# Gate and up products of two FFNs as seven block products each, with their result kept in DRAM until the down product

## The chip, the cores and the metric
One core of a Trainium2 chip runs the whole program in one launch. The metric is device time in microseconds. The kernel before took 2929.18 us (median of three runs, 2927.11 to 2929.26).

## The reference
Two transformer blocks on 1024 tokens of width 1024, all in float32. Each has a mixer (block 1: sliding-window attention and an mLSTM; block 2: retention and an indexed sparse attention), an output projection with norm and residual, and an FFN with a hidden width of 2816. Only the FFNs, and the projections that lead into them, are touched:

```python
# block 1
mix = merged @ w_out;  x = x + gate_m * rms_norm(mix, g_post_mix)
h2 = modulate(rms_norm(x, g_pre_ffn), shift_f, scale_f)
ff = (silu(h2 @ w_ffn_gate) * (h2 @ w_ffn_up)) @ w_ffn_down
x = x + gate_f * rms_norm(ff, g_post_ffn)
# block 2
h = h + rms_norm(mixed, g_post)
up = causal_dwconv(rms_norm(h, ffn_norm_pre) @ w_up, conv_w, conv_b)   # three taps along the tokens
g, u = split(up);  ffn = (silu(g) * u) @ w_down
h = h + rms_norm(ffn, ffn_norm_post)
```

## The kernel before
A dense product splits each float32 operand into two float32r parts (hi + lo) and adds hi*hi, hi*lo and lo*hi in one PSUM bank: three matmuls for each block of 128 contracted features (mm3, L129 to L133). Weights come from DRAM as units of 1 MB into one raw buffer; ScalarE copies the high part (L643) and GpSimd subtracts it to make the low part (L645), in pieces of 512 columns, some steps ahead of their use. There is one raw buffer, so the load of a unit (L631) waits for the last split of the unit before.

TensorE, VectorE, ScalarE and GpSimd each run their instructions in the order in which the program writes them ("steps": a slot emits its matmuls, and work put off from earlier slots is emitted between slots). DMAs are issued by SyncE, also in order. PSUM has four banks for products (pd), three (pa) for transposes and other results, and one more.

`dense` (L164) serves both blocks. The output projection goes slot by slot, 24 matmuls of 256 columns each: a slot is a unit of columns and a token block of 128. Once a token block has its four units, `residual` (L203) adds it to x (L209), squares it on ScalarE, takes a power on GpSimd (L148), and scales it (L217); in block 1 GpSimd then adds a shift row (L219). `turn` (L225) transposes the eight 128x128 blocks of a token block on TensorE (L157); ScalarE and VectorE split the result (L160, L161).

The FFN has 22 gate/up units of 128 gate and 128 up features. `gate_up` makes for each unit, for two halves of 512 tokens, the gate and the up product: 8 blocks x 3 matmuls of 512 columns each. In block 1 ScalarE takes the Silu (L304) and VectorE multiplies (L305); in block 2 `convolve` comes first, half by half, with two taps on VectorE (L295, L296). The hidden result is split (L306, L307) and stays in SBUF. After every two units follows `down`: 8 token blocks x 2 column halves x 6 matmuls, added to an accumulator in SBUF by VectorE (L338). So gate/up and down alternate. The ends of the phases (the last down groups, the norms, the projection of the next phase) are written out by hand.

Of the kernel before, what the change touches and what calls it, by code (L numbers as in the profile page):

```python
# [35 lines left out]
# Rows of the table of row vectors.  # L36
# [3 lines left out]
# Columns of the table of per-feature columns.  # L40
# [15 lines left out]
# 2 * pi in pieces: products of the first four with integers below 2 ** 16 are exact.  # L56
# [8 lines left out]
def pipeline(n, stages):  # L65
    """Emit stage k of item i together with stage 0 of item i + k, older items first (None: a step of delay)."""
# [6 lines left out]
class Steps:  # L73
    """Work put off to later steps of an emission loop."""
# [12 lines left out]
class Builder:  # L87
# [54 lines left out]
    def rstd(self, pool, ssum, n, width, eps=EPS):  # L142
        """(ssum / n + eps) ** -0.5 for a [P, width] tile."""
# [7 lines left out]
    def transpose_split(self, x, tbl, big, kt0, nkt):  # L151
        """nkt [P, P] blocks of x transposed into kt0.. of big [P, 2, KT, HALF] at token block tbl."""
# [11 lines left out]
    def dense(self, pool, bigs, held, w0, names, x_src, x_mid, x_dst, rows, rows2, conv, ahead=None):  # L164
        """x_mid = x_src + norm(X @ W) * row; x_dst = x_mid + norm(down(act(gate, up))) * row, a step at a time.

        held: results of the output projection's first unit that are in PSUM already.  ahead: (unit of weights,
        function) of the next phase's first projection, which covers the end of this phase; the unit after it.
        Returns the next norm's transposed parts and the weights of that unit."""
        nc = self.nc  # L170
        steps = Steps()
        W = {("o", i): w for i, w in enumerate(w0)}
# [1755 lines left out]
```

## Time and profile before

| | us |
|---|---|
| median of three runs | 2929.18 |
| the profiled execution: span from the first to the last instruction | 2928.6 |
| TensorE busy in it | 2816.4 |
| VectorE, ScalarE, GpSimd busy in it | 1347.1, 1084.4, 1183.2 |

Of the profiled execution the profile gives the span; the runs are timed apart, and their median is 0.6 us above it. The output projection of block 1 runs from about 730 to 809 us of the span and its FFN to about 1537; those of block 2 from about 2123 to 2195 and to the end. In the profile PE is TensorE's matmuls, PEld its weight loads, DVE VectorE, ACT ScalarE, POOL GpSimd and SP SyncE. A busy PE means that matmuls are in flight, not that each is at its peak rate. A line L645 is line 645 of the kernel; helpers such as mm3 have the lines of many callers.

### The profile page before, as it was taken

Reading aid. Unit: us, or ns where it says so; the run is one execution under the profiler, and the core shown is the slowest. Engines: PE = TensorE matmul, PEld = TensorE weight load, DVE = VectorE, ACT = ScalarE, POOL = GpSimd, SP = SyncE. Lnnn points to the kernel's source line nnn. Section 1 sums busy time; section 2 is a strip of 40 time slices with the busy share of each in tenths; the row PEclk is TensorE's granted clock in tenths of the full one; section 3 lists DMA queues with packets and bytes.
Section 4 is the critical chain, followed back from the end, with each engine's and each line's share of the span. In section 5 each row is a group of like instructions: output and inputs, shape, how many; then the busy total and the mean of one; then the engine's idle time right before and its main releaser. Section 6 shows DMA issues by size and latency. Waiting matters only on the chain. (4 is left out here: it accounts for less than half of the span.)

```text
span 2928.6 us, 41049 instructions
## 1 busy us (share of the span) xinstructions
PE 2816.4 (96%) x16152; PEld 2441.9 (83%) x16152; DVE 1347.1 (46%) x2618; ACT 1084.4 (37%) x2294; POOL 1183.2 (40%) x1217
## 2 busy tenths in 40 slices
PE   5899999999999999999998999989999999999999
PEld 4898888888978888888878999978897888888887
DVE  8645434532522222111135787786444444444446
ACT  5653213232331111111123767747534322333333
POOL 5652222244443322232346444568433433333345
PEclk7999999999999999999999999999999999999999
DMA  6112343253321111111123111111131111111113
GB/s 206 39 36 103 105 165 105 96 192 130 116 94 58 57 44 44 43 46 56 44 79 108 44 43 41 49 58 45 52 124 58 51 58 44 44 43 58 44 44 144
DMA packets 67815, 220.15 MB, mean 75 GB/s; under 512 B 7159, under 2 KB 26615, under 8 KB 53542
## 3 DMA queue, kind: packets, MB, share of 16 engines
q1 hardware_dynamic: 67622, 217.53, 21.1%
q8 instruction: 127, 2.08, 0.3%
q14 instruction: 66, 0.54, 0.1%
HBM read 183.93 MB, written 33.57 MB: 74 GB/s over the span
## 5 line engine op out<-in xcount | busy, mean ns | idle before, releaser
L645 POOL TENSOR_TENSOR wlo<-raw,whi 128x512 fp32r<-128x512 f32 (+1 forms) x426 | 570.1, 1358 | 375.9 <-ACT whi L643 375.1
L131 PE MATMUL pd<-big,whi 128*128 128x512 f32 x1792 | 703.5, 393 | 0.0
L133 PE MATMUL pd<-big,wlo 128*128 128x512 f32 x1792 | 698.0, 390 | 1.7 <-POOL wlo L645 1.7
L132 PE MATMUL pd<-big,whi 128*128 128x512 f32 x1792 | 697.5, 389 | 0.0
L131 PE MATMUL pd<-whi,big 128*128 128x256 f32 (+1 forms) x1728 | 504.1, 292 | 8.0 <-ACT whi L643 3.6
L132 PE MATMUL pd<-wlo,big 128*128 128x256 f32 (+1 forms) x1728 | 494.2, 286 | 8.2 <-POOL wlo L645 8.2
L133 PE MATMUL pd<-whi,big 128*128 128x256 f32 (+1 forms) x1728 | 493.1, 285 | 0.9 <-POOL big L582 0.6
L133 PEld LDWEIGHTS pd<-big,wlo 128*128 128x128 f32 x1792 | 336.4, 188 | 73.2 <-POOL wlo L645 2.6
L131 PEld LDWEIGHTS pd<-big,whi 128*128 128x128 f32 x1792 | 336.6, 188 | 70.0 <-issue 1.2
L132 PEld LDWEIGHTS pd<-big,whi 128*128 128x128 f32 x1792 | 336.6, 188 | 70.0 <-issue 1.4
L307 POOL TENSOR_TENSOR hid<-sg,hid 128x512 fp32r<-128x512 f32 x88 | 113.9, 1295 | 619.1 <-ACT hid L306 619.1
L132 PEld LDWEIGHTS pd<-wlo,big 128*128 128x128 f32 x1728 | 335.8, 194 | 10.9 <-POOL wlo L645 9.9
L131 PEld LDWEIGHTS pd<-whi,big 128*128 128x128 f32 x1728 | 335.3, 194 | 11.4 <-ACT whi L643 4.5
L133 PEld LDWEIGHTS pd<-whi,big 128*128 128x128 f32 x1728 | 335.2, 194 | 1.4 <-POOL big L582 0.9
L338 DVE TENSOR_TENSOR big<-big,pd 128x512 f32<-128x512 f32 x304 | 206.3, 686 | 176.2 <-PE pd L133 176.1
L132 PE MATMUL pd<-wlo,hid 128*128 128x512 f32 x704 | 277.6, 394 | 0.0
L131 PE MATMUL pd<-whi,hid 128*128 128x512 f32 x704 | 276.8, 393 | 0.0
L133 PE MATMUL pd<-whi,hid 128*128 128x512 f32 x704 | 273.5, 388 | 0.0
L643 ACT ACTIVATE whi<-raw 128x512 fp32r<-128x512 f32 (+1 forms) x428 | 246.0, 621 | 15.9 <-DMA raw<-in_wu 15.9
L305 DVE TENSOR_TENSOR sg<-sg,pd 128x512 f32<-128x512 f32 x44 | 30.2, 687 | 432.9 <-PE pd L133 432.9
L295 DVE SCALAR_TENSOR_TENSOR cv<-craw,cols,cv 128x512 f32<-128x512 f32 x88 | 87.3, 992 | 290.4 <-ACT cv L294 187.1
L289 ACT ACTIVATE craw<-pd 128x512 f32<-128x512 f32 x88 | 52.7, 599 | 351.1 <-PE pd L133 349.4
(375 smaller groups left out, 3986.7 us busy)
## 6 DMA issues: line engine op xcount, KB each, us to landing
raw<-in_wu SPq DMA_DIRECT2D x109, 1024.0 KB, 4.9
row<-in_w_ada SPq DMA_DIRECT2D x32, 512.0 KB, 3.8
x_d<-xin SPq DMA_DIRECT2D x24, 512.0 KB, 2.6
ada<-in_w_ada SPq DMA_DIRECT2D x16, 512.0 KB, 8.0
xin<-x_d SPq DMA_DIRECT2D x16, 512.0 KB, 3.3
big<-in_x SPq DMA_DIRECT2D x8, 512.0 KB, 4.8
tga_d<-tg SPq DMA_DIRECT2D x16, 256.0 KB, 2.2
tgm_d<-tg SPq DMA_DIRECT2D x16, 256.0 KB, 2.0
```

What stands on the lines that cost most here:

```text
L131: mm(ps, lh, rh, start=start, stop=False)
L132: mm(ps, lh, rl, start=False, stop=False)
L133: mm(ps, ll, rh, start=False, stop=stop)
L289: nc.scalar.activation(raw[:, 2:], ps, AF.Copy)
L295: nc.vector.scalar_tensor_tensor(cv, raw[:, 1 : 1 + HALF], wc[1], cv, op0=ALU.mult, op1=ALU.add)
L305: nc.vector.tensor_mul(sg, sg, u)
L307: nc.gpsimd.tensor_tensor(out=lo, in0=sg, in1=hi.bitcast(F32), op=ALU.subtract)
L338: nc.vector.tensor_add(a, a, ps)
L643: nc.scalar.activation(w[0][:, c], raw[:, c], AF.Copy)
L645: eng.tensor_tensor(out=w[1][:, c], in0=raw[:, c], in1=w[0][:, c].bitcast(F32), op=ALU.subtract)
```

## The change
The tokens are taken as even and odd token blocks, the 1024 contracted features as two halves, the outputs as gate and up. That makes 2 x 2 blocks, whose product Winograd's form of Strassen's method needs in seven block products in place of eight. Weights keep their unit of 1 MB, but laid out as four quarters.

* `combine` makes in place, for a pair of token blocks, the four combinations of the tokens' side; `turn_block` transposes and splits one block of one of the seven left operands (a pair has seven such blocks of four transposes each). They are emitted in the last slots of the output projection and the first of the FFN. Combinations of the first three pairs are GpSimd's, of the last VectorE's. Some go through DRAM (`t_d`).
* `prep` makes one of the seven weight operands of a unit: sums on VectorE, the high part on ScalarE, the low part on GpSimd or (three of seven in block 2) VectorE. Operands are made up to six slots ahead.
* `multiply` makes one product, 4 x 3 matmuls of 512 columns. Products 1 and 2 share a PSUM bank (A), as do 6, 7 and 4 (B), and 5 and 3 (Z): later ones are added to the earlier. `after_product` (emitted at the start of the next slot) takes what the bank holds then.
* The first unit makes products 1, 3 and 2 in two halves of 256 columns, and uses one more bank.
* In block 2 the convolution runs over all 1024 tokens of the unit before.
* The hidden result goes to DRAM (`h_d`). All down groups follow after the last unit; each loads its two hidden blocks and splits them.

```diff
+        def combine(p, eng):
+            e, o = yrow[2 * p], yrow[2 * p + 1]
+            e1, e2, o1, o2 = e[:, :HALF], e[:, HALF:], o[:, :HALF], o[:, HALF:]
+            for out, a, b in ((e1, o1, e1), (o1, o2, o1), (o2, o2, e1), (e2, e2, o2)):
+                eng.tensor_tensor(out=out, in0=a, in1=b, op=ALU.subtract)
...
+        def prep(f, m, eng):
...
+            def total(a, b, op):
+                t = px.tile([P, HALF], F32, tag="ws", bufs=3, name="ws")
+                nc.vector.tensor_tensor(out=t, in0=a, in1=b, op=op)
+                return t
+            if m in (6, 5, 3) and (f, 5) not in sums:
+                sums[f, 5] = sub(a21, a22, ALU.add)
+                sums[f, 6] = sub(sums[f, 5], a11)
+            if m == 3:
+                sums[f, 3] = sub(a12, sums[f, 6])
+            if m == 7:
+                sums[f, 7] = sub(a11, a21)
...
+            nc.scalar.activation(w[:, 0], s, AF.Copy)
+            eng.tensor_tensor(out=w[:, 1], in0=s, in1=w[:, 0].bitcast(F32), op=ALU.subtract)
...
+        def multiply(f, m, c, special):
+            b = {1: "A", 2: "A", 6: "B", 7: "B", 4: "B", 5: "Z", 3: "Y" if special else "Z"}[m]
...
+        def after_product(f, m, special, c):
...
+            if m == 1:
...
+                nc.scalar.activation(t["t1"][:, c], A[:, c], AF.Copy)
+            elif m == 6:
+                t["u2"] = temp()
+                plus(t["u2"], t["t1"], B)
...
+            elif m == 7:
+                t["w"] = temp()
+                plus(t["w"], t["t1"], B)
+                if conv:
+                    plus(odd(raws[1][:, 2:]), four(t["w"]), four(Z))
+                else:
+                    plus(t["w"], t["w"], Z)
...
+            elif m == 2:
+                if conv:
+                    nc.scalar.activation(even(raws[0][:, 2:]), four(A), AF.Copy)
+                else:
+                    t["sg"] = temp()
+                    nc.scalar.activation(t["sg"], A, AF.Silu)
+            elif m == 3 and not special:
+                c12(f)            # u2 + Z: to raws[0], or (block 1) in place and Silu
+                if not conv:
+                    product(f, 1)     # on GpSimd, and to DRAM
+            elif m == 4:
+                if conv:
+                    plus(even(raws[1][:, 2:]), four(t["t1"]), four(B))
+                else:
+                    plus(t["t1"], t["t1"], B)
+                    product(f, 0)     # on VectorE, and to DRAM
...
+        def conv_taps(f, j):
...
+            for i in (1, 0):
+                nc.vector.scalar_tensor_tensor(cv, raws[j][:, i : i + S], wc, cv, op0=ALU.mult, op1=ALU.add)
+            if j == 0:
+                nc.scalar.activation(cv, cv, AF.Silu)
...
+        order = (1, 6, 5, 7, 2, 3, 4)
...
+        for f in range(1, NF):
+            pre = [[] for _ in range(7)]
+            if conv:
+                g = f - 1
+                pre[0] += [lambda g=g: conv_start(g, 0)]
+                pre[1] += [lambda g=g: conv_taps(g, 0), lambda g=g: conv_start(g, 1)]
+                pre[2] += [lambda g=g: conv_taps(g, 1)]
+                pre[3] += [lambda g=g: conv_end(g)]
...
+                pre[0] += [q(f, 3, v if conv else nc.gpsimd), q(f, 4)]
+            if f + 1 < NF:
+                pre[1] += [lambda f=f: raw_load(f + 1)]
+                for i in range(5):
+                    pre[2 + i] += [q(f + 1, order[i], v if conv and i in (2, 4) else nc.gpsimd)]
...
+            run([slot(f, m, pre[i]) for i, m in enumerate(order)])
```

In a slot of this loop, first what follows on the product before is emitted, then the entries of `pre`, then the slot's matmuls. `q` is `prep`, with GpSimd for the low part unless another engine is given.

## Rows read from the trace of the kernel before

**Rows 1.** The page: busy time of TensorE, its busy tenths, and its granted clock.
```profile
PE 2816.4 (96%) x16152; PEld 2441.9 (83%) x16152; DVE 1347.1 (46%) x2618; ACT 1084.4 (37%) x2294; POOL 1183.2 (40%) x1217
...
PE   5899999999999999999998999989999999999999
...
PEclk7999999999999999999999999999999999999999
```
**Rows 2.** Busy time by stretches: bounds, length, each engine's busy us, clock, DMA.
```profile
773.00:809.00 36.00, 28.65 (x239) 27.70 (x237) 27.97 (x37) 14.13 (x36) 18.93 (x16) 1.00 0.39 147
809.00:835.00 26.00, 22.06 (x108) 17.73 (x107) 16.57 (x21) 12.33 (x24) 16.06 (x11) 1.00 0.46 162
1098.00:1171.00 73.00, 73.00 (x323) 60.26 (x322) 15.63 (x23) 11.29 (x20) 20.19 (x16) 1.00 0.13 44
2195.00:2222.00 27.00, 24.15 (x118) 19.76 (x117) 16.93 (x25) 15.24 (x29) 9.47 (x15) 1.00 0.28 98
2342.00:2416.00 74.00, 74.00 (x327) 61.06 (x326) 33.58 (x43) 21.11 (x36) 24.39 (x30) 1.00 0.16 57
```
**Rows 3.** Instructions in order of time, VectorE, first FFN: start, length, what.
```profile
1002.29 0.69 DVE L305 TENSOR_TENSOR sg<-sg,pd 128x512 f32<-128x512 f32 x1 [10.19 <-PE pd L133]
1013.17 0.69 DVE L305 TENSOR_TENSOR sg<-sg,pd 128x512 f32<-128x512 f32 x1 [10.19 <-PE pd L133]
```
**Rows 4.** In order of time, TensorE, end of the second output projection.
```profile
2187.16 1.04 PE L157 MATMUL pa<-ident,big 128*128 128x128 f32 x8
2187.95 0.36 PE L131 MATMUL pd<-whi,big 128*128 128x256 f32 x1
...
2193.78 1.04 PE L157 MATMUL pa<-ident,big 128*128 128x128 f32 x8
```
**Rows 5.** In order of time, GpSimd, second FFN.
```profile
2263.81 2.99 POOL L645 TENSOR_TENSOR wlo<-raw,whi 128x512 fp32r<-128x512 f32 x2
...
2272.38 5.06 POOL L645 TENSOR_TENSOR wlo<-raw,whi 128x512 fp32r<-128x512 f32 x4 [0.21 <-ACT whi L643]
...
2403.28 5.08 POOL L645 TENSOR_TENSOR wlo<-raw,whi 128x512 fp32r<-128x512 f32 x4
...
2435.89 2.54 POOL L645 TENSOR_TENSOR wlo<-raw,whi 128x512 fp32r<-128x512 f32 x2
...
2438.51 2.99 POOL L645 TENSOR_TENSOR wlo<-raw,whi 128x512 fp32r<-128x512 f32 x2
```
**Rows 6.** In order of time, GpSimd, first turn into the FFN.
```profile
802.01 2.43 POOL L219 TENSOR_TENSOR big<-big,row 128x1024 f32<-128x1024 f32 x1 [1.50 <-DVE big L217]
```
**Rows 7.** Groups by line and shape, whole span: count, busy us, mean ns, idle before.
```profile
L643 ACT ACTIVATE whi<-raw 128x512 fp32r<-128x512 f32 x424 | 243.8, 621 | 15.9 <-DMA raw<-in_wu 15.9
L294 ACT ACTIVATE cv<-pd,cols 128x512 f32<-128x512 f32 x88 | 68.2, 775 | 0.0
L148 POOL TENSOR_TENSOR rs_r<-rs_v,mhalf 128x1 f32<-128x1 f32 x56 | 35.5, 641 | 77.1 <-DVE rs_v L146 77.1
L304 ACT ACTIVATE sg<-cv 128x512 f32<-128x512 f32 x44 | 27.8, 632 | 0.0
L198 ACT ACTIVATE junk<-xin 128x1024 bf16<-128x1024 f32 x24 | 25.4, 1057 | 39.8 <-DVE xin L209 35.3 <-DVE rs_v L146 4.3
```
**Rows 8.** In order of time, VectorE, end of the kernel.
```profile
2892.01 0.69 DVE L395 TENSOR_TENSOR yout<-big,row 128x512 f32<-128x512 f32 x1
...
2894.10 2.41 DVE L384 SCALAR_TENSOR_TENSOR big<-yout,rs_r,big 128x1024 f32<-128x1024 f32 x1
...
2898.96 1.29 DVE L384 SCALAR_TENSOR_TENSOR big<-yout,rs_r,big 128x1024 f32<-128x1024 f32 x1
```
**Rows 9.** In order of time, VectorE, second FFN.
```profile
2401.03 2.50 DVE L338 TENSOR_TENSOR big<-big,pd 128x512 f32<-128x512 f32 x4
2404.21 0.69 DVE L338 TENSOR_TENSOR big<-big,pd 128x512 f32<-128x512 f32 x1 [0.69 <-PE pd L133]
...
2438.60 1.76 DVE L295 SCALAR_TENSOR_TENSOR cv<-craw,cols,cv 128x512 f32<-128x512 f32 x1 [4.70 <-POOL craw L288]
2440.39 1.66 DVE L296 SCALAR_TENSOR_TENSOR cv<-craw,cols,cv 128x512 f32<-128x512 f32 x1
2442.51 0.75 DVE L295 SCALAR_TENSOR_TENSOR cv<-craw,cols,cv 128x512 f32<-128x512 f32 x1 [0.45 <-ACT cv L294]
```
**Rows 10.** In order of time, GpSimd, end of the kernel.
```profile
2894.12 1.31 POOL L395 TENSOR_TENSOR yout<-big,row 128x512 f32<-128x512 f32 x1
...
2899.04 2.38 POOL L395 TENSOR_TENSOR yout<-big,row 128x512 f32<-128x512 f32 x1
```
**Rows 11.** In order of time, SyncE's queue, second FFN.
```profile
2266.83 10.96 SPq L631 DMA_DIRECT2D raw<-in_wu  x2
```
**Rows 12.** In order of time, ScalarE, second FFN.
```profile
2271.67 2.20 ACT L643 ACTIVATE whi<-raw 128x512 fp32r<-128x512 f32 x4 [0.88 <-DMA raw<-in_wu]
```

More of the change, by code (lines that the diff above doesn't have):

```diff
@@ new lines, in dense @@
+        banks, tt = {}, {}
+        even = lambda x: x.rearrange("p (b e t) -> p b e t", e=2, t=P)[:, :, 0]
+        odd = lambda x: x.rearrange("p (b e t) -> p b e t", e=2, t=P)[:, :, 1]
+        four = lambda x: x.rearrange("p (b t) -> p b t", t=P)
+        def multiply(f, m, c, special):
+            b = {1: "A", 2: "A", 6: "B", 7: "B", 4: "B", 5: "Z", 3: "Y" if special else "Z"}[m]
+            first = (f, b) not in banks or special and m in (1, 3)
+            if (f, b) not in banks:
+                banks[f, b] = self.ps() if b == "B" else self.pd()
+            ps, w, x = banks[f, b], wq[f, m], X[m]
+            for k in range(4):
+                lh, ll = w[:, 0, k * P : (k + 1) * P], w[:, 1, k * P : (k + 1) * P]
+                for i, (l, r) in enumerate(((lh, x[:, 0, k, c]), (lh, x[:, 1, k, c]), (ll, x[:, 0, k, c]))):
+                    nc.tensor.matmul(ps[:, c], l, r, start=first and k == 0 and i == 0, stop=k == 3 and i == 2, skip_group_check=True)
@@ new lines, in c12, with product @@
+        def c12(f):
+            t, Z = tt[f], banks[f, "Z"]
+            if conv:
+                plus(odd(raws[0][:, 2:]), four(t["u2"]), four(Z))
+            else:
+                plus(t["u2"], t["u2"], Z)
+                nc.scalar.activation(t["u2"], t["u2"], AF.Silu)
+        def product(f, o):
+            t = tt[f]
+            h, u = (t["u2"], t["w"]) if o else (t["sg"], t["t1"])
+            (nc.gpsimd if o else nc.vector).tensor_tensor(out=h, in0=h, in1=u, op=ALU.mult)
+            nc.sync.dma_start(h_d[f, :, o * HALF : (o + 1) * HALF], h)
@@ L260, in dense, with conv_end @@
+        def conv_end(f):
+            g, u = tt[f]["cv", 0], tt[f]["cv", 1]
+            nc.vector.tensor_tensor(out=g, in0=g, in1=u, op=ALU.mult)
+            nc.sync.dma_start(h_d[f], g)
         for tb, ps in held.items():
@@ new lines, in dense, with slot, body @@
+        calls[3, 6] = [lambda: combine(1, nc.gpsimd), q(0, 3)]
+        calls[3, 7] = [d(3, 2), d(1, 2)]
+        run([(lambda s=s: ([fn() for fn in calls.get(s, ())], proj(*s)())) for s in slots])
+        lo, hi = slice(0, 256), slice(256, HALF)
+        post = []
+        def slot(f, m, pre=(), c=slice(0, HALF), special=False):
+            def body():
+                for fn in post:
+                    fn()
+                post.clear()
+                for fn in pre:
+                    fn()
+                multiply(f, m, c, special)
+                post.append(lambda: after_product(f, m, special, c))
+            return body
@@ new lines, in dense, with hid_piece, first_hidden @@
+        eso.close()
+        if conv:
+            pools["v"] = self.pool(eso, name + "v")
+        order = (1, 6, 5, 7, 2, 3, 4)
+        groups, hidden = {}, {}
+        def hid_piece(f, c, hraw, eng):
+            hi, lo = (hidden[f][:, i, c * HALF : (c + 1) * HALF] for i in range(2))
+            s = hraw[:, c * HALF : (c + 1) * HALF]
+            nc.scalar.activation(hi, s, AF.Copy)
+            eng.tensor_tensor(out=lo, in0=s, in1=hi.bitcast(F32), op=ALU.subtract)
+        def first_hidden():
+            t = self.bigtile([P, 4, 2, S], F32R)
+            for i in range(4):
+                hidden[i] = t[:, i]
@@ L405, in dense @@
             fetch("dn", g[1], (2, 2, 3, 3))
-            run([lambda tb=tb: both(g[:1], tb) for tb in range(4)] + [lambda tb=tb, c=c: slot(tb, c) for tb in range(NT) for c in range(2)])
+            run([lambda tb=tb: both(g[:1], tb) for tb in range(4)] + [lambda tb=tb, c=c: last(tb, c) for tb in range(NT) for c in range(2)])
+            eso.close()
             return None, None
@@ L441, in dense @@
         assert not steps.due
+        eso.close()
         return nxt, W[then]
```

300 lines of the change are left out of this document (200 added, 100 removed).

## The prediction
> **What bounds the kernel now.** I read the page first. TensorE is busy for 96% of the span, and its row of forty slices shows 9s nearly throughout [rows 1]. Then the busy time by stretches: in the middle of either FFN, TensorE is busy for the whole stretch, while VectorE has 15.6 of 73 us in the first FFN and 33.6 of 74 in the second, ScalarE 11 to 21 and GpSimd 20 to 24 [rows 2]. So an FFN lasts as long as its matmuls are many, and the other engines seem to have room. Where an output projection turns into an FFN there is idle time on TensorE: 7.4 and 3.9 us in the two stretches around the first turn, 2.9 us at the second [rows 2]. The granted clock is 1.00 (of 2.4 GHz) in all five stretches, so I leave it out of the sum. The question is whether the change keeps the other engines off TensorE's path.
>
> **Matmuls removed.** A gate/up unit has 2 x 2 x 8 x 3 = 96 matmuls of 512 columns now. Two halves of a unit start 10.88 us apart [rows 3], so 48 matmuls take 10.88 us, 0.2267 each. After the change a unit has 7 x 4 x 3 = 84, that is 19.04 us for 21.76: 2.72 us less. For 44 units: **-119.7 us**. The down product's matmuls stay as many.
>
> **Matmuls added.** The transposes grow from 64 to 7 x 4 x 4 = 112 for each FFN. Eight take 0.79 us [rows 4], so 96 more cost **+9.5**. The first unit does three products in two halves of 256 columns; such a matmul takes 0.12 us (48 and a start-up in 5.83 us [rows 4]): 72 x 0.12 - 36 x 0.2267 = 0.5 for each FFN, **+1**.
>
> **The turns into the FFNs.** The pairwise combinations are new: 4 operations for each pair of token blocks, three pairs on GpSimd. One operation on 128x512 costs it 1.27 us (four in 5.08 [rows 5]), so 5.1 a pair. In the first FFN GpSimd also adds the shift, 2.4 us a token block [rows 6], in the same in-order queue. From the slot in which the first combination is issued until token block 5 has its shift, the queue holds three shifts (7.2), two combinations (10.2), two weight splits (2.5), four powers (0.6 each by their group in [rows 7], 2.4) and three waits for VectorE's scaling (1.3 or more each, [rows 8]): some 27 us. TensorE wants that block five slots of 2.9 us and their transposes later, at 15.7: it waits 11. Block 7 follows behind the third combination and two splits, some 6 us more, and block 3 costs 1. That is 18 for the 11.3 idle there now, +7; in the second FFN, without shifts, the same count gives 7.5 for 2.9, +4.6. Each turn also has bursts of up to five block transposes, 0.4 us on TensorE against 0.62 for VectorE's half of the split, +2 each. **+16**; from below 0 (GpSimd only gets work added ahead of these transposes, so no gain), from above all six combinations laid bare, 31.
>
> **The waits inside a unit.** This decides the case. Product 5 lies alone in PSUM bank Z, product 3 is added to the same bank, and in between VectorE must read Z (after_product of 7). TensorE comes to product 3 five slots of 2.72 us after the unit's start, at 13.6. When is VectorE through? It works in the order written.
> *Prices.* On VectorE, an addition with one operand in PSUM takes 0.69 us, four in a row 0.62 apart, also while GpSimd works (the additions from 2403.3 on, [rows 5, 9]); two SBUF operands cost 0.69 at 512 columns and 1.28 at 1024 [rows 8, 9]. ScalarE takes 0.62 for a split's high part, 1.06 for 1024 columns [rows 7], and about 1.2 for scale and bias on 1024: 0.775 for 512 [rows 7] and the 0.43 by which the 1024 form exceeds the 512 one. Where VectorE has two SBUF operands and GpSimd works, one of them stands still: 1.76 and 1.66 for 0.75 on VectorE beside two splits on GpSimd [rows 5, 9], 2.41 for 1.29 on VectorE, and the other way 2.38 for 1.31 on GpSimd [rows 8, 10]. I call that a collision: 0.95 us on VectorE in the first pair, 1.1 in the other; I take 1.1.
> The Trainium skill ("SBUF — State Buffer", section "Who interferes with whom") says that VectorE with two SBUF inputs and GpSimd contend for one pair of ports, an exclusive lock that is held for the whole instruction. By it a collision could cost the full 1.27 instead of 1.1, two of them in each unit 0.34 more, 7 us over the second FFN; the rows show the loser blocked, at less than the full price.
> *Second FFN (convolution).* In order: addition for product 4 from 0.2 (drain), sum for product 3 ending at 1.5, ScalarE's high part 2.2, VectorE's low part (queued behind it), first two taps (1.28 each) ending at 5.45. Then ScalarE, in its order, does the Silu and only after it the start of the other convolution: 1.06 + 1.16, so VectorE's next taps begin at about 7.8 and end at 10.4; conv_end 11.6; two dependent sums 13.0; the addition of B 13.65, that of Z 14.35. That is 0.8 behind 13.6. Two GpSimd splits fall into it: that of product 4 is ready just as the first tap is, and that of the next unit's product 1 (raw weights landed at about 9.1) comes during the second pair of taps. Nothing but VectorE's SBUF work covers them: 2.2 more. Stall 3.0 a unit, 21 units: **+63**. Below: no collision, 0.8 x 21 = 17; above: one collision more in each unit, 4.1 x 21 = 86.
> *First FFN.* GpSimd makes all seven low parts and a product. Its last split of a unit ends about 6.0 after the unit's start: silu-product and one split from the slot before, to 1.4; VectorE's product, held by the lock, and a sum to 2.8; ScalarE 3.45; two splits 6.0. That frees the one raw buffer; the load goes out at once (GpSimd ends at 2266.80, issue 2266.83) and ScalarE reads it 4.84 us later [rows 5, 11, 12]: 10.9. Two dependent sums, B and Z follow: 13.7, a stall of 0.1; but the split of product 1 becomes ready (10.9 + 0.71, ScalarE's start to GpSimd's in [rows 5, 12]) just when the second sum does (10.9 + 0.69 + the 0.03 that lie between the two taps of [rows 9]), and if GpSimd goes first the stall is 1.3. I take 0.8, with 20 units: **+16**; bounds 2 and 26.
>
> **Edits at no cost.** The store of the hidden blocks and their reload (22 x 0.5 MB each way and FFN) lie beside matmuls: the DMA share is 0.13 in the middle of the FFN [rows 2]. Without that cover a reload costs about the 4.84 of the twice larger weight block, for 22 blocks of each FFN 213 us in all at most. In the down phase a group has 96 matmuls, 21.8 us, for 16 additions at 0.62 and two or four splits on VectorE (at most 14 us), and six on GpSimd (7.6); VectorE may wait for a late block some 3 us, and four PSUM banks of 1.36 us cover that.
>
> **Sum**, against the profiled execution, whose span is 2928.6 (the median of the runs shown, 2929.2, is 0.6 above it, which I carry over): 2929.2 - 119.7 + 9.5 + 1 + 16 + 63 + 16 = 2915; I say **2914**.
>
> **Rivals.**
> *The stall is bare* (2855). The collisions fall where VectorE waits or has a PSUM operand. For it: most of VectorE's additions in the present FFNs pass GpSimd's splits unharmed [rows 5, 9]. Against: the changed queue is nearly all SBUF work. -119.7 + 10.5 + 16 + 17 + 2 = -74.
> *All the product's saving* (2835): VectorE is through before 13.6 everywhere, as its mean load suggests [rows 2]: -119.7 + 10.5 + 16. Against it: the Silu standing between the two convolution starts.
> *Slower* (2948): the wait on Z in the second FFN. At 3.7 us a unit, (119.7 - 10.5 - 16 - 16) / 21, it eats the whole gain. One more collision, of the split of product 6 or 7 once everything is late, makes 4.1: 86, with the first FFN at 1.3 a unit (26): -119.7 + 10.5 + 16 + 86 + 26 = +19. For it: the rows where both engines lose, 2.99 for two splits that take 2.54 [rows 5]. Against: that of product 6 becomes ready only when VectorE turns to PSUM.
>
> **Chances.** Forecast 50% (own range 2895 to 2932), bare stall 22%, all the saving 8%, slower 20%. A measurement of this kernel can tell about 0.2%, 6 us, from no change. Of the forecast's half, 0.38 is below 2923, 0.09 within, 0.03 above; the two faster rivals add 0.30, the slower one 0.02 to within and 0.18 to above. The range, 2845 to 2945, takes in the bare stall and the lower half of the slower case, and leaves out the full saving and the slower case's upper end.
>
> **What would show it.** In the second FFN a unit takes about 22 us, not 19, and TensorE's matmuls of product 3 wait for VectorE's addition of Z; VectorE's taps show 2.3 us beside GpSimd's splits. In the first FFN a unit takes 19.1 or 20.3, with the same wait, and VectorE's first sum waits for the raw weights' DMA. TensorE idles about 18 and 7.5 us at the turns. I am wrong if product 3 starts without a wait, or if TensorE waits for hidden blocks in the down phase.

## The result, and the profile after

The changed kernel takes 3031.82 us (median of four runs, 3030.13 to 3032.05), the kernel before 2929.22 in the same comparison (2927.11 to 2930.19). The ratio is 1.035, 95% interval 1.0336 to 1.0365: slower by 103 us, where 15 less were forecast. The profiled execution's span is 3028.4 us.

The page of the changed kernel: busy time, TensorE's busy tenths and the granted clock (against [rows 1]).
```profile
PE 2781.1 (92%) x15792; PEld 2391.7 (79%) x15792; DVE 1750.1 (58%) x3026; ACT 1151.1 (38%) x2364; POOL 1272.1 (42%) x1155
...
PE   5899999999679999999989999889968998998999
...
PEclk7999999999889999999999999999989999998999
```
TensorE has 360 matmuls fewer and is busy for 35 us less, where they were worth 109 net: part of its work runs slower. The tenths fall in slices 11 and 12 and in slice 30 (the turns), and in places in the second FFN (slices 31, 34 and 37). The busy time by stretches answers to [rows 2] (bounds, length, each engine's busy time, clock, DMA):
```profile
780.00:820.00 40.00, 20.49 (x152) 20.08 (x151) 27.01 (x33) 9.75 (x26) 28.31 (x20) 0.79 0.33 118
820.00:860.00 40.00, 27.12 (x168) 25.63 (x166) 24.71 (x33) 17.33 (x33) 16.44 (x12) 0.78 0.29 106
1098.00:1171.00 73.00, 69.16 (x300) 55.67 (x299) 33.26 (x38) 21.10 (x38) 39.77 (x30) 1.00 0.19 71
2195.00:2222.00 27.00, 16.78 (x121) 16.40 (x119) 18.18 (x25) 7.84 (x22) 19.31 (x15) 0.84 0.43 152
2222.00:2276.00 54.00, 39.98 (x234) 34.84 (x235) 33.14 (x47) 21.55 (x43) 19.45 (x18) 0.86 0.22 79
2342.00:2416.00 74.00, 66.21 (x267) 53.24 (x268) 52.16 (x55) 27.67 (x40) 17.58 (x14) 0.93 0.20 72
```
In the middle of the FFNs (third and last line) TensorE is no longer busy throughout. In the turns it is busy for half to three quarters, at a granted clock of 0.78 to 0.86. What TensorE waited for (us in total, times, longest):
```profile
PE pd L374 <- DVE craw L377: 59.2, 21, 6.6
PE pd L374 <- DVE wt L377: 23.1, 21, 2.6
PE pa L300 <- POOL big L239: 21.8, 3, 11.9
PE pa L300 <- DVE big L304: 20.8, 9, 3.7
...
PE pa L300 <- DVE big L237: 12.4, 2, 7.6
```
L374 is the matmul of `multiply`, L377 the addition of `plus`, L300 the transpose of a token block, L239 and L237 the shift and the scaling of its residual, L304 the split's low part. The first two rows are product 3's wait for bank Z, in the second and the first FFN: the wait of the prediction. Laid out by stages, from points that both traces have: the last merge before a projection, the start of unit 1, the first down product. In the kernel before, units 0 and 1 are interleaved and three units lie ahead of the first down product (at 881.9 and 2266.2); there the turn is taken to end two bare units, 43.5 us, ahead of it. So the waits inside these units count to the turn, as they did in the forecast.

| stage | before | after | difference | predicted |
|---|---|---|---|---|
| first turn: projection and unit 0 | 131.0 | 172.9 | +41.9 | +11.6 |
| first FFN, units 1 to 21 | 457.0 | 432.9 | -24.1 | -41 |
| second turn: projection and unit 0 | 116.7 | 150.6 | +33.9 | +9.1 |
| second FFN, units 1 to 21 | 457.0 | 493.3 | +36.3 | +6 |
| all else (+10.5 of it behind the second FFN's last unit) | | | +11.8 | 0 |

The profiled executions differ by 99.8 us, where the forecast's terms add up to -14. Of these 114 us that the forecast lacks, 55 lie in the turns, 30 in the second FFN, 17 in the first and 12 elsewhere, most of them in the down phase.

### The profile page after: what moved, and what is told of

It reads as the page before. It is cut to its first block, busy times and chain, and to the rows that moved or that the text cites. A ratio compares the mean times of both kernels' runs of the same rounds, so it can differ in the third digit from the quotient of the medians.

```text
span 3028.4 us, 41525 instructions
## 1 busy us (share of the span) xinstructions
PE 2781.1 (92%) x15792; PEld 2391.7 (79%) x15792; DVE 1750.1 (58%) x3026; ACT 1151.1 (38%) x2364; POOL 1272.1 (42%) x1155
## 4 chain that ended last, share of the span: by engine, by line
PE 54%; DVE 19%; POOL 9%; ACT 8%; issue 6%; DMA 4%; SPq 0%; DVEq 0%; ACTq 0%; POOLq 0%
PE pd L131 12%; PE pd L132 12%; PE pd L133 12%; PE pd L374 5%; DVE cv L445 5%; PE pa L374 4%; DMA raw<-in_wu 4%; ACT tk_junka L1647 2%; DVE ws L343 2%; POOL whi L357 2%; POOL wlo L357 2%; DVE wt L377 1%; POOL wlo L909 1%; DVE craw L377 1%; POOL wx L357 1%
## 5 line engine op out<-in xcount | busy, mean ns | idle before, releaser
L131 PE MATMUL pd<-whi,big 128*128 128x256 f32 (+2 forms) x1856 | 557.4, 300 | 11.8 <-DVE big L570 3.7
L132 PE MATMUL pd<-wlo,big 128*128 128x256 f32 (+2 forms) x1856 | 546.4, 294 | 8.1 <-POOL wlo L909 8.1
L133 PE MATMUL pd<-whi,big 128*128 128x256 f32 (+2 forms) x1856 | 545.4, 294 | 0.9 <-POOL big L846 0.6
L909 POOL TENSOR_TENSOR wlo<-raw,whi 128x512 fp32r<-128x512 f32 (+1 forms) x254 | 350.7, 1392 | 405.5 <-ACT whi L907 405.0
L131 PE MATMUL pd<-big,whi 128*128 128x512 f32 x448 | 180.3, 402 | 0.0
L445 DVE SCALAR_TENSOR_TENSOR cv<-craw,cols,cv 128x1024 f32<-128x1024 f32 x88 | 156.4, 1778 | 37.6 <-ACT cv L437 36.0
L133 PE MATMUL pd<-big,wlo 128*128 128x512 f32 x448 | 175.0, 391 | 0.3 <-POOL wlo L909 0.3
L132 PE MATMUL pd<-big,whi 128*128 128x512 f32 x448 | 174.6, 390 | 0.0
L374 PE MATMUL pd<-big,whi 128*128 128x512 f32 (+1 forms) x672 | 162.0, 392 | 1.9 <-ACT big L303 1.4
L374 PE MATMUL pa<-big,wlo 128*128 128x512 f32 x648 | 159.7, 395 | 4.2 <-ACT big L303 2.8
L374 PE MATMUL pa<-big,whi 128*128 128x512 f32 x624 | 151.5, 392 | 1.7 <-DVE wt L377 1.7
L374 PEld LDWEIGHTS pa<-big,wlo 128*128 128x128 f32 x648 | 123.7, 191 | 31.9 <-ACT big L303 3.3
L374 PEld LDWEIGHTS pd<-big,whi 128*128 128x128 f32 x672 | 127.3, 197 | 27.2 <-ACT big L303 1.9
```

The costliest lines, as they stand in the source:

```text
L131: mm(ps, lh, rh, start=start, stop=False)
L132: mm(ps, lh, rl, start=False, stop=False)
L133: mm(ps, ll, rh, start=False, stop=stop)
L374: nc.tensor.matmul(ps[:, c], l, r, start=first and k == 0 and i == 0, stop=k == 3 and i == 2, skip_group_check=True)
L445: nc.vector.scalar_tensor_tensor(cv, raws[j][:, i : i + S], wc, cv, op0=ALU.mult, op1=ALU.add)
L909: eng.tensor_tensor(out=w[1][:, c], in0=raw[:, c], in1=w[0][:, c].bitcast(F32), op=ALU.subtract)
```

## The experiments: the wait inside a unit

One unit of the second FFN in the changed kernel, TensorE, then VectorE, ScalarE (start, length, what, and in brackets the idle time before and who ended it):
```profile
2412.64 3.06 PE L374 MATMUL pd<-xq,whi 128*128 128x512 f32 x12 [2.42 <-DVE craw L377]
...
2434.55 4.60 PE L374 MATMUL pd<-xq,wlo 128*128 128x512 f32 x12 [2.53 <-DVE craw L377]
...
2457.92 4.61 PE L374 MATMUL pd<-xq,wx 128*128 128x512 f32 x12 [2.42 <-DVE craw L377]
```
```profile
2421.12 3.70 DVE L445 SCALAR_TENSOR_TENSOR cv<-craw,cols,cv 128x1024 f32<-128x1024 f32 x2
...
2427.08 3.51 DVE L445 SCALAR_TENSOR_TENSOR cv<-craw,cols,cv 128x1024 f32<-128x1024 f32 x2 [1.66 <-ACT cv L437]
2430.62 1.22 DVE L451 TENSOR_TENSOR cv<-cv 128x1024 f32<-128x1024 f32 x1
2431.77 0.68 DVE L343 TENSOR_TENSOR ws<-raw 128x512 f32<-128x512 f32 x1
2432.49 0.69 DVE L343 TENSOR_TENSOR ws<-ws,raw 128x512 f32<-128x512 f32 x1
2433.09 0.68 DVE L377 TENSOR_TENSOR wt<-wt,pa 128x512 f32<-128x512 f32 x1
2433.81 0.69 DVE L377 TENSOR_TENSOR craw<-wt,pd 128x512 f32<-128x512 f32 x1
```
```profile
2424.85 1.06 ACT L447 ACTIVATE cv<-cv 128x1024 f32<-128x1024 f32 x1 [3.08 <-DVE cv L445]
2425.82 1.23 ACT L437 ACTIVATE cv<-craw,cols 128x1024 f32<-128x1024 f32 x1
```
The granted clock of two units, the first at its full rate, the next with the longer product:
```profile
2412.00:2434.00 22.00, 19.38 (x84) 15.69 (x84) 16.77 (x18) 8.77 (x13) 5.39 (x5) 1.00 0.20 73
2434.00:2458.00 24.00, 21.03 (x85) 16.91 (x85) 17.16 (x19) 9.18 (x14) 5.97 (x5) 0.93 0.19 66
```
The rows above are the predicted chain, link by link: taps, Silu, the other convolution's start, taps, product, two sums, two additions; TensorE begins when the last ends. Two things are to be seen besides: two taps take 3.5 to 3.7 us for 2 x 1.28, and the product after the wait takes 4.60 us at 2434.55, though the same product took 3.06 at 2412.64, behind nearly the same wait. The theory was that this chain costs what the trace shows and that standing still lowers the clock; the rivals are in the expectations.

**A bank for product 3.** It uses the fourth bank (Y) in every unit, and Z is added right behind product 7:
```diff
-            b = {1: "A", 2: "A", 6: "B", 7: "B", 4: "B", 5: "Z", 3: "Y" if special else "Z"}[m]
+            b = {1: "A", 2: "A", 6: "B", 7: "B", 4: "B", 5: "Z", 3: "Y"}[m]
...
+                if not special:
+                    plus(t["u2"], t["u2"], Z)
...
```


> Product 3 gets a PSUM bank of its own, and VectorE adds product 5 to the partial sum earlier (one more addition of 0.69 us a unit), so TensorE no longer has to wait until bank Z is read. Theory (TensorE waits for VectorE's reading of Z, 0.9 us a unit in the first FFN and 2.5 in the second, and its clock falls in the second FFN because it stands still): the waits before product 3 vanish, a unit takes 19.1 to 19.4 us in the first FFN (20.4 now), and in the second what VectorE itself needs, 19.3 to 20.5 (23 now), at a clock of 1.00; 2930 to 2965 us in all. Rival (VectorE's throughput or PSUM is the bound, the wait on Z only where it shows): the wait moves to another product, second-FFN units stay above 21.5, and the time above 3000.

Measured 2943.34 us, ratio to before 1.0052 (1.0029 to 1.0075): 88 us back. Of the first FFN only the last unit still waits (0.63 us). In the second a shorter wait for the same late VectorE remains, now in front of product 4's bank (0.76 to 0.99 us a unit but at the ends), and a unit takes 20.4.

**The convolution's start first.** ScalarE starts the second convolution before VectorE's first taps, so that the Silu no longer stands in between:
```diff
-                pre[1] += [lambda g=g: conv_taps(g, 0), lambda g=g: conv_start(g, 1)]
+                pre[1] += [lambda g=g: conv_start(g, 1), lambda g=g: conv_taps(g, 0)]
```


> Only the order of two lines: ScalarE starts the second half of the convolution before the Silu of the first. Theory (VectorE stands still some 1.7 us a unit until ScalarE has done Silu and start, and that lies on the way to Z): the wait before product 3 in the second FFN falls from 2.5 to 0.8 us, a unit from 21.9 or 23.4 to 20.2 with the clock back at 1.00; 2965 to 2985 us. Rival (collisions with GpSimd or VectorE's total work set it): the wait stays above 2, and the gain under 15 us.

Measured 2973.07, ratio 1.0153 (two runs): 59 us from one line. The wait is 25.3 us in 21 (0.80 to 1.07 each but the ends), and the granted clock from 2300 to 2700 is 1.00.

**GpSimd's splits out of the chain.** From the third unit of the second FFN on, ScalarE copies the low parts of operands 1 and 4 (left out: their subtraction), so GpSimd leaves VectorE's taps alone:
```diff
+            if conv and f > 1 and m in (1, 4):
+                nc.scalar.activation(w[:, 1], s, AF.Copy)
+            else:
```


> Left out: in the second FFN from the third unit on the low parts of the weight operands of products 1 and 4, for which ScalarE writes a copy, so GpSimd does not work beside the taps. Theory (each of these splits blocks VectorE for 1.0 to 1.2 us): two taps take 2.6 us in place of 3.5 to 3.7, the wait before product 3 falls from 2.5 to 0.2 to 0.6, a unit to 19.5 to 20; 2955 to 2975 us. Rival (the taps are long by themselves, or the wait comes from the Silu alone): taps and wait unchanged within 0.3, the gain under 10 us.

Measured 2970.27, ratio 1.0144 (two runs). The wait is 19.4 us in 21, 0.46 to 0.53 each but the ends, and every pair of taps but those at the ends takes its bare time:
```profile
2412.08 2.61 DVE L448 SCALAR_TENSOR_TENSOR cv<-craw,cols,cv 128x1024 f32<-128x1024 f32 x2 [1.32 <-ACT cv L440]
```
So the two collisions make up 2.0 us of the 2.5.

**The wait filled.** Ten matmuls whose result is not used, ahead of product 3 in the second FFN:
```diff
+            if conv and m == 3 and not special:
+                dump = self.psp.tile([P, 512], F32, tag="py", bufs=1, name="py")
+                for i in range(10):
+                    nc.tensor.matmul(dump, wq[f, 2][:, 0, :P], X[2][:, 0, i % 4, :], start=True, stop=True)
```


> Added: ten matmuls of 512 columns on a spare PSUM bank before product 3 of every unit of the second FFN but the first, 2.27 us, read by nobody. Theory (the clock falls because TensorE stands still): they fit into the 2.5 us wait, the clock stays at 1.00, every unit takes 21.9 and none 23.4, and the kernel becomes faster by about 20 us, to 3005 to 3015, though it computes more. Rival (the clock falls for another reason): units of 23.4 stay, the time is the same or up to 45 us longer.

Measured 3007.95, ratio 1.0273 (two runs): 24 us faster than the changed kernel, with more work. The same 300 us of the second FFN, changed kernel and then with the wait filled (clock third from the end):
```profile
2400.00:2700.00 300.00, 267.81 (x1102) 215.75 (x1101) 217.73 (x223) 111.93 (x156) 69.52 (x53) 0.95 0.19 69
```
```profile
2400.00:2700.00 300.00, 297.00 (x1294) 241.43 (x1293) 228.47 (x235) 118.84 (x165) 74.12 (x55) 1.00 0.20 74
```
With TensorE's waits filled every unit but the first and last takes 21.8 to 21.9 us and none 23.4. So the clock falls because TensorE stands still, and that costs at least those 24 us.

**Bank and start together.** The first two edits.

> Both edits of the first pair together: product 3 has a PSUM bank of its own, and ScalarE starts the second convolution before VectorE's first taps. If each took away its part of one wait, product 3 of the second FFN no longer waits, the granted clock there is 1.00, and a unit takes 19.1 to 19.6 us where it took 20.4 with the bank alone: 21 x 0.8 to 1.3 = 17 to 27 us under 2943, so 2916 to 2926. If the wait on the scaled temporary (0.76 to 0.99 us a unit with the bank alone) has another cause than the late convolution, it stays: 2938 to 2944. The two turns stay as long as in the changed kernel in either case.

Measured 2913.85, ratio 0.9949 (0.9932 to 0.9965): faster than the kernel before. From the third on a unit of the second FFN takes 19.04 us, 84 x 0.2267, without a wait. The kernels below build on this one. Against the sum without stalls, 2929.2 - 119.7 + 10.5 = 2820, 94 us are left: by the stages of the table some 71 in the turns, 7 in the units and the rest in the down phases and what follows them.

## The experiments: the turns

TensorE at the first turn of the changed kernel (projection matmuls left out):
```profile
792.45 1.97 PE L300 MATMUL pa<-ident,big 128*128 128x128 f32 x8 [7.58 <-POOL big L239]
...
819.33 1.97 PE L300 MATMUL pa<-ident,big 128*128 128x128 f32 x8 [11.93 <-POOL big L239]
...
825.59 1.66 PE L374 MATMUL pd<-big,wx 128*128 128x256 f32 x12
...
833.14 0.66 PE L300 MATMUL pa<-ident,big 128*128 128x128 f32 x4 [3.59 <-DVE big L304]
837.48 1.11 PE L300 MATMUL pa<-ident,big 128*128 128x128 f32 x4 [3.68 <-DVE big L304]
838.24 2.91 PE L374 MATMUL pd<-big,whi 128*128 128x256 f32 x12
```
The 7.6 and the 12 us are waits for the shifts of token blocks 3 and 5; later ones are for a PSUM bank that VectorE's split has not yet freed. Some products run at half the clock: 2.91 us for 1.66, with a granted clock of 0.50 from 838.2 to 841.0. GpSimd before the shift of block 5 has the split, the combination and the split that the prediction counted, the first two at greater lengths:
```profile
802.29 2.41 POOL L239 TENSOR_TENSOR big<-big,row 128x1024 f32<-128x1024 f32 x1 [1.40 <-DVE big L237]
804.66 2.29 POOL L357 TENSOR_TENSOR wx<-raw,wx 128x512 fp32r<-128x512 f32 x1
806.91 6.39 POOL L311 TENSOR_TENSOR big<-big 128x512 f32<-128x512 f32 x4
813.25 1.26 POOL L357 TENSOR_TENSOR wx<-ws,wx 128x512 fp32r<-128x512 f32 x1
814.47 1.06 POOL L148 TENSOR_TENSOR rs_r<-rs_v,mhalf 128x1 f32<-128x1 f32 x2
816.94 2.34 POOL L239 TENSOR_TENSOR big<-big,row 128x1024 f32<-128x1024 f32 x1 [1.40 <-DVE big L237]
```

**Combinations left out, transposes later, waits filled.** Three kernels:
```diff
             for out, a, b in ((e1, o1, e1), (o1, o2, o1), (o2, o2, e1), (e2, e2, o2)):
-                eng.tensor_tensor(out=out, in0=a, in1=b, op=ALU.subtract)
+                pass
```


> On top of the run with both edits (2916 to 2926). Left out: the subtractions of the pairwise combinations, so products 5, 6, 7 and 4 take blocks that are not combined; transposes, stores and reloads stay. Theory 'GpSimd's combinations hold the transposes back' (the step of the prediction): the waits on L239 and L304 in the turns shrink by 20 to 28 us over both, so some 2892 to 2905. Theory 'the transposes are placed too early behind their residual, and VectorE's and TensorE's own pace sets the rest': only the collisions go, under 8 us.


```diff
-        calls[3, 5] = [d(3, 1), d(1, 1)]
...
+        calls[3, 6] = [d(3, 1), d(1, 1), q(0, 3)]
+        calls[2, 7] = [d(2, 1)]
...
+            slot(0, 3, [d(3, 2), d(1, 2), q(0, 5)], lo, True),
```


> On top of the run with both edits (2916 to 2926). The transposes of token blocks 2 to 5 are emitted two slots later, those of blocks 4 and 5 in the first unit's slots; nothing is left out. Theory 'placed too early': TensorE's waits of 7.6 and 11.9 us in the first turn and of 4.8 and 7.6 in the second go, and as everything behind the waiting transposes moves up too, 18 to 30 us are gained: 2888 to 2906. Theory 'GpSimd and VectorE are the bound of the turn': the same wait comes back on token blocks 4 to 7 in the first unit, less than 8 us gained.


```diff
+        calls[3, 5] = [lambda: dummy(30), d(3, 1), d(1, 1)]
...
+        calls[3, 7] = [lambda: dummy(46), d(3, 2), d(1, 2)]
```


> On top of the run with both edits (2916 to 2926). Added: matmuls whose result is not used, 30 and 46 of 512 columns ahead of the transposes that wait longest and 24, 24 and 16 of 256 columns ahead of waiting transposes in the first unit, at each turn; they fill the time in which TensorE stands still and lengthen no chain as long as they are no longer than the wait. If the halved clock costs its own share of the turns, the granted clock stays near 1.00 in both and 10 to 22 us are gained; if the turns last as long as VectorE's and GpSimd's chains and the clock only makes TensorE's part of a wait look busy, nothing changes or up to 10 us are lost, above all in the second turn, where the waits are shorter than the filling.

Measured, from 2913.85: 2893.65 without the combinations (-20.2), 2909.28 with later transposes (-4.6), 2909.86 filled (-4.0); the last two are not clear of noise. Filling took the clock of the stretch 780 to 820 from 0.78 to 0.99 and that of 820 to 860 from 0.80 to 0.88, yet unit 0's last product starts at 875.72 instead of 875.66, and the two turns last 172.3 and 150.3 us for 172.8 and 151.2: the clock costs them next to nothing, TensorE's slow work lies beside another chain. Moving the transposes took the 12 us wait away and brought another in its place, for the bank:
```profile
831.46 1.75 PE L300 MATMUL pa<-ident,big 128*128 128x128 f32 x7 [10.30 <-DVE xq L304]
```

**The turn in another order, and GpSimd emptied.** First all of the turn re-ordered as the expectation says, then also the shift on VectorE, then the combinations and the first weight splits there too:
```diff
+        calls[3, 5] = [co(0, 0)]
+        calls[3, 6] = [d(3, 1), d(1, 1), co(0, 1)]
...
+            slot(0, 5, [d(5, 3), d(6, 3), q(0, 4)], lo, True),
+            slot(0, 5, [d(7, 0), d(4, 0), lambda: raw_load(1)], hi, True),
```


> On top of the run with both edits (2913.9). Only the order of the turn's work is changed: no transposes of token blocks 4 and 5 between the projection's slots and those of 2 and 3 two slots later; GpSimd's subtractions issued singly, behind the powers and shifts; the first weight blocks split some slots earlier; products 5 and 7 of the first unit in two halves, and each transpose a slot ahead of the product that reads it. Theory 'the transposes close a loop over the in-order queues (TensorE waits for a residual, which stands on VectorE behind a split that waits for TensorE's earlier transposes, and on GpSimd behind combinations and weight splits)': without the loop the projection ends some 20 us earlier in the first turn and unit 0 ends 25 to 45 us earlier, in the second turn 15 to 30: 2840 to 2875. Theory 'VectorE's and GpSimd's volume of work sets the turns, in whatever order': under 15 us in all, so over 2899.


```diff
-                        (nc.vector if out else nc.gpsimd).tensor_tensor(out=o, in0=o, in1=shift, op=ALU.add)
+                        nc.vector.tensor_tensor(out=o, in0=o, in1=shift, op=ALU.add)
```


> On top of the reordered turn (2898.5). Only the first turn is changed: VectorE adds the shift of all token blocks, where GpSimd added that of the first six. In the reordered turn VectorE's residual (L228) takes 2.3 to 3.3 us beside GpSimd's shift, 1.28 without it, and the chain of a token block's residual advances by 8 us for the projection's 5.8. Theory 'two SBUF operands on VectorE beside GpSimd stand still, and that holds the chain': L228 takes 1.28, the chain follows the projection, and 6 to 14 us are gained: 2884 to 2893. Theory 'volume on VectorE': the 6 x 1.28 us that it gets cost what the collisions give back, within 3 us of 2898.5.


```diff
+        co = lambda p, *ops: lambda: combine(p, nc.vector, ops)
```


> As the run with the shift on VectorE, and in both turns the three combinations and the first unit's weight splits move from GpSimd to VectorE too, so that GpSimd has only the powers there. Theory 'collisions': VectorE's operations with two SBUF operands take their bare 0.69 and 1.28 throughout both turns, and another 6 to 18 us are gained over both: 2870 to 2886. Theory 'volume': VectorE gets 19 more operations of 0.69 us in each turn, 13 us, of which the collisions give back about half: 5 to 15 us lost against the run with the shift alone.

Measured 2898.47 (0.9895, 0.9878 to 0.9911), 2905.17 and 2894.55 (0.9882, 0.9863 to 0.9902). The order is worth 15 us, just past the bound of the volume theory and far from the 39 to 74 of the other. The collisions are real: VectorE's residual in the re-ordered turn, and with GpSimd emptied,
```profile
802.10 3.32 DVE L228 SCALAR_TENSOR_TENSOR xin<-big,rs_r,xin 128x1024 f32<-128x1024 f32 x1
```
```profile
813.17 1.28 DVE L228 SCALAR_TENSOR_TENSOR xin<-big,rs_r,xin 128x1024 f32<-128x1024 f32 x1
```
(the first beside GpSimd's shift),
```profile
801.92 2.41 POOL L239 TENSOR_TENSOR big<-big,row 128x1024 f32<-128x1024 f32 x1 [1.40 <-DVE big L237]
```
but taking them away gained 4 us in all, which is not clear of noise. The shift alone lost 7, more than either theory had. The second step gained 11 on that, within the 6 to 18 that the collision theory had for it, where the volume theory had 5 to 15 lost. So neither theory holds by itself: in sum, what the collisions gave back, VectorE's added work took.

**Rows early.** The transposes of token blocks 4 to 7 read rows of blocks 0 to 3 (left out: that they are the right ones), in the second kernel also without the combinations:
```diff
-            s = xt[p][:, (m == 4) * HALF : (m == 4) * HALF + HALF] if m in (7, 4) and p in xt else block(m, p)
+            e = p % 2
+            s = xt[e][:, (m == 4) * HALF : (m == 4) * HALF + HALF] if m in (7, 4) and e in xt or p == 3 and m > 4 else block(m, e)
```


> On top of the run with both edits (2913.9). Changed: the transposes of token blocks 4 to 7 read the rows of blocks 0 to 3, which are there early; all instructions stay as many, on the same engines, in the same order. Theory 'latency without cover': TensorE stands behind the residuals of late token blocks, for which the first unit has 4.3 us of products ready where the kernel before had two half units of 10.9; without that dependence the projection ends 12 us earlier, unit 0 follows in some 30 us, and 50 to 65 us are gained over both turns: 2850 to 2864. Theory 'volume of VectorE and GpSimd': they have the same work, so less than 25 us are gained: over 2889.

> As the run with early rows, and without the subtractions of the combinations, which alone gained 20.2 us. Theory 'latency': their 20 us were part of the late blocks' chain, so here they are worth 0 to 8 us more. Theory 'volume': they are worth 15 to 25 us here too.

Measured 2910.32 and 2891.27: -3.5, which is not clear of noise, and -19.1 more. My theory of a bare latency fell: TensorE's wait for the late shift only became one for a bank,
```profile
822.82 1.54 PE L301 MATMUL pa<-ident,big 128*128 128x128 f32 x6 [9.98 <-DVE xq L305]
```
and the bank waits for the steps of a late residual in two queues. VectorE's addition of the residual (L228) is long beside the shift, ScalarE's square (L217) waits for it, and behind the square stand ScalarE's high part of the split and VectorE's low part:
```profile
817.06 3.25 DVE L228 SCALAR_TENSOR_TENSOR xin<-big,rs_r,xin 128x1024 f32<-128x1024 f32 x1
822.07 0.69 DVE L305 TENSOR_TENSOR xq<-pa,xq 128x512 fp32r<-128x512 f32 x1 [1.76 <-ACT xq L304]
```
```profile
820.40 1.06 ACT L217 ACTIVATE junk<-xin 128x1024 bf16<-128x1024 f32 x1 [2.69 <-DVE xin L228]
...
821.46 0.58 ACT L304 ACTIVATE xq<-pa 128x512 fp32r<-128x512 f32 x1
```
**The last residual issued earlier**, on the kernel with GpSimd emptied. In the same kernel the third combination and the later weight splits go back to GpSimd, and product 1's copy is issued earlier:
```diff
-                    residual(tb, mix[:, tb, :], self.rstd(pools["c"], ss, D, 1), lambda: xin, x_mid, arow, shift, (1, 1, 0.5),
+                    residual(tb, mix[:, tb, :], self.rstd(pools["c"], ss, D, 1), lambda: xin, x_mid, arow, shift, (0.5, 0.5, 0.5) if tb >= NT - 2 else (1, 1, 0.5),
```

> On top of the turn with GpSimd emptied (2894.6). The residual of token blocks 6 and 7 is issued half a slot earlier at each step, ahead of subtractions and splits in VectorE's queue; product 1's copy is issued on ScalarE right behind the product, ahead of a token block's square; the third combination and the later weight splits go back to GpSimd, where no residual is left. If the last block's residual is what the turn waits for, both turns end 3 to 7 us earlier: 2880 to 2889. If VectorE's work behind that block is the bound, it stays within 4 us of 2894.6.

Measured 2894.51 (0.9885, 0.987 to 0.9899): no gain on 2894.55, as expected if VectorE's work is the bound; with several edits in one kernel a gain and a loss could also have cancelled.

**The queues emptied.** On the kernel with early rows, the low parts of transposed blocks leave VectorE; or the residual of blocks 4 to 7 leaves all queues; or this and the combinations:
```diff
-            nc.vector.tensor_sub(lo, v, hi.bitcast(F32))
+            nc.scalar.activation(lo, v, AF.Copy)
```


> On top of the run with early rows (2910.3). Left out: VectorE's low parts of the transposed blocks; ScalarE copies the block once more instead. So nothing of VectorE's queue stands between a PSUM bank and the next transposes. Theory 'the splits wait in VectorE's queue behind the residual, and so the banks': 15 to 35 us are gained over both turns, 2875 to 2895. If ScalarE's queue holds the banks as well (its square of a token block waits for VectorE's residual and stands ahead of the copies), less than 10 us.


```diff
                 x = xin()
+                if out is not None and tb >= 4:
+                    nc.sync.dma_start(dst[tb * P : (tb + 1) * P, :], x)
...
+                    return
```


> On top of the run with early rows (2910.3). Left out: the residual and norm of token blocks 4 to 7 (addition, square, powers, scaling, shift; the loaded row is stored as it came), so that neither VectorE's nor ScalarE's nor GpSimd's queue has them between the splits; the projection, the combinations, transposes and splits all stay. Theory 'the queues of the residual hold the turn': with them and the dependence gone 35 to 60 us are gained over both turns, 2850 to 2875. Theory 'the added work itself (28 blocks to split, combinations, weight sums) is as long as the turn': less than 20 us.

> As the run without the late blocks' residual (2875.0), and without the subtractions of the combinations too. If the two add up (GpSimd's combinations and VectorE's residual are separate volumes in front of the first unit), another 14 to 22 us are gained: 2853 to 2861, and some 60 of the turns' 85 us are accounted for. If the combinations only cost where the residual is late, less than 6 us.

Measured 2895.07 (-15.2), 2875.01 (-35.3), 2859.02 (-16.0 more). The first is at the low end of its theory's range, and the longest wait for a bank is still there, now for ScalarE alone:
```profile
820.83 2.09 PE L301 MATMUL pa<-ident,big 128*128 128x128 f32 x8 [9.72 <-ACT xq L305]
```
So VectorE's queue is one part of it, and ScalarE's, with the squares of the late blocks, holds the banks as well. The two prices add up: the late residuals 39 us (3.5 as a dependence, 35.3 as work in the queues), the combinations 16 to 20. Together 55 of the 94 us, and 53 of the 71 in the turns.

Why did the same residuals cost so little before? The last projection matmul, the first FFN product and the last transposes, TensorE before; and the last shift, GpSimd before:
```profile
806.33 0.28 PE L133 MATMUL pd<-whi,big 128*128 128x256 f32 x1
...
808.95 0.48 PE L131 MATMUL pd<-big,hid 128*128 128x512 f32 x1
...
831.95 1.04 PE L157 MATMUL pa<-ident,big 128*128 128x128 f32 x8
```
```profile
827.21 2.43 POOL L219 TENSOR_TENSOR big<-big,row 128x1024 f32<-128x1024 f32 x1 [1.16 <-DVE big L217]
```
Token block 7 was ready 23 us after the projection ended; in the changed kernel it is 18 (825.2 to 843.1). But 22 us of products on token blocks 0 to 3, the first halves of units 0 and 1 (`run(a[:4] + b[:4] + a[4:])`), lay there, and TensorE went on. The changed kernel has three half products, 4.3 us, and three more splits for each pair of blocks (28 in all for 16), the combinations and the weight sums in the same queues. That the cover is gone is read from these rows; a kernel with the cover put back was not run.

## Why the prediction was wrong

**Matmuls removed, added: right.** Without waits a unit takes 19.04 us in the second FFN and 19.1 to 19.2 in the first. **Stores and reloads: nearly right.** What follows the second FFN's last unit takes 10.5 us longer than before. TensorE waits there once,
```profile
PE pd L131 <- DVE big L570: 3.7, 1, 3.7
```
not for a hidden block but for VectorE's first copy out of a bank, which four banks had been thought to cover; and 864 of its down matmuls come 0.233 us apart, where those of the kernel before come 0.229 (96 in 21.98 from 2790.10 on).

**The wait on Z: right in place and chain.** Forecast 3.0 us a unit in the second FFN and 0.8 in the first; shown 2.42 to 2.57 and 0.76 to 1.25, but for the first and last units. The bare chain was put at 0.8 and is 0.5 without GpSimd's splits. A collision was priced at 1.1 us; the taps show 0.95 and 1.14. The Trainium skill ("SBUF — State Buffer", "Who interferes with whom") has the port pair locked for a whole instruction, so that the loss would grow with the other's length. The taps lose somewhat less than a split's 1.29, but L228 beside a shift of 2.4 us loses 2.0: the trace agrees in kind, and one price for every pair was wrong. The kernel before had the dearer pair already: the same addition (there L209) took 3.31 to 3.35 us in five of the eight token blocks of the first turn, 1.28 in the others.

**The clock: missing.** "The granted clock is 1.00 (of 2.4 GHz) in all five stretches, so I leave it out of the sum" is the step that failed in the second FFN. It was read from a kernel in which TensorE did not stand still in the middle of an FFN, and kept for one in which it was to wait 3 us in each unit. A unit takes 21.9 us at a clock of 1.00 and 23.4 at 0.93, three of four the longer: 14 x 1.5 = 21 us, and the first and last waits (6.6 and 5.6 us) 7 more: nearly all of the 30 us. In the first FFN a mean wait of 1.1 (23.1 us in 21) goes with a period of 20.6, 1.5 over the bare one. Of that 0.3 is more wait than forecast, and some 0.4 is the refill: the last product before a wait lasts 2.88 us instead of the 2.72 after which the next would start, and the one behind it takes 2.9 until the next starts.

**The turns: mis-sized by 55 us.** "+16" counted GpSimd's queue up to one block, with a subtraction at its bare 1.27 (6.39 us for four are shown, not 5.1). The wait for token block 5 was put at 11 us and is 11.93; but that for block 3, put at 1, is 7.58, and the waits for a bank, put at 2 a turn, are 2.2 to 3.7 each. In all TensorE waits 38.6 and 24.2 us in the two turns, for 18 and 7.5 (and twice 2) in the forecast. VectorE's queue, which carries residual, splits, sums and additions, was counted only as those 2 us, ScalarE's squares not at all; nor was it counted that the transposes have three banks, free only when ScalarE and VectorE have both read them, nor that the first units of the kernel before had 22 us of work that needs no late block. The upper bound of 31 came from GpSimd's queue alone, so the range could not hold the result. The rival that turned out slower was named for the wrong reason: it took the wait on Z at 4.1 us, and that was 2.5.

What stays open: of the 94 us, 39 are left when the late residuals and the combinations are both left out. Some 18 of them lie in the turns, 7 in the units and 13 elsewhere, most in the down phases; no run takes them apart.

## What to carry to other kernels

When an algorithm mixes blocks, ask what the first result now needs: work that could start on half of the input may have been the cover of the stage before, and that cover is part of the price. In such a stage add up each in-order queue in full, VectorE's and ScalarE's too, and count the PSUM banks between them and TensorE; removing one wait there only shows the next. A wait on TensorE of a few us in each unit has a second price, the clock, and a third, the refill. Here one more bank and one exchanged line were worth 118 us, and turned +3.5% into -0.5%; with the turn re-ordered and GpSimd emptied it is -1.2%.

## What the runs showed of the hardware

* Behind waits of 2.42 to 2.57 us, one in each unit, twelve matmuls took 4.2 to 4.6 us in three units of four, with a granted clock of 0.61 from 2434.6 to 2439.0, between the levels of 1.2 and 2.4 GHz. In the fourth they took 3.0 to 3.1 at a clock of 1.00. With waits of 0.80 to 1.07 us a unit it stayed at 1.00. A wait of 2.42 us went by once without a loss (at 2412.64) and once with it (at 2457.92), and waits of 2.3 and 3.3 us in the first turn of the kernel before went by at 1.00 [rows 2]: a single wait's length does not decide it.
* TensorE with ten useless matmuls a unit was faster than TensorE waiting, by 24 us.
* An operation of 1.28 us on VectorE, with two operands in SBUF, took 3.25 to 3.32 beside GpSimd's 2.4 us shift, and 1.28 again when GpSimd had none.
* Two operations of 1.28 us took 3.5 to 3.7 beside one GpSimd split of 1.3 to 1.45, and 2.6 when there was none.
